# One of four weight sums of a seven-product pair moved from VectorE to an accumulating transfer, with one raw tile less

## The chip, the cores and the metric

The kernel runs on one core of a Trainium2 chip. The metric is the device time of one execution in microseconds (us). The engines are called by the profile's names: PE is TensorE (PEld its weight loads), DVE is VectorE, ACT is ScalarE, POOL is GpSimd, and SP is the engine that issues most transfers.

## The reference, cut to what matters

One layer of a decoder on 256 tokens of width 2048 in float32. Attention and a state-space branch come first; the change lies in the feed-forward part, whose matrices hold most of the weights:

```python
hf = rms_norm(x, g_ffn_norm[i])                                     # 256 x 2048
x = x + (jax.nn.silu(hf @ w_gate[i]) * (hf @ w_up[i])) @ w_down[i]  # 2048 x 5632, twice, and 5632 x 2048
gate = jax.nn.sigmoid(rms_norm(x, g_ple_norm[i]) @ w_ple_gate[i])   # 2048 x 2048
x = x + gate * (p[i] @ w_ple_proj[i])
```

## The kernel before, in words

**Products.** PE multiplies in a rounded 32-bit format. To keep the accuracy, each weight tile and each activation is split into a rounded part `hi` and the rest `lo`, and each product is made of three matmuls (hi by hi, hi by lo, lo by hi). ACT makes `hi` by a copy, DVE makes `lo` by a subtraction (lines 200 and 201).

**Weights.** The class `Weights` holds one list of tiles ("chunks") of 256 rows by 512 columns, 512 KB each, in the order in which PE needs them. `load_to` issues their loads on SP's queue (line 174), `split_to` makes `hi` and `lo`, and `take` hands a chunk to PE while it splits three chunks ahead and loads as many more as there are raw tiles. A raw tile `w_raw` comes from a ring of five; in the gate and up stage two more, `w_more`, take their turn at chunk numbers that leave 0 or 3 after division by seven, so that seven tiles rotate until block 8. A raw tile comes free when ACT and DVE have read it, and only then can SP issue the next load into it.

**Gate and up stage.** There are 11 blocks of 512 columns. A block goes over eight pairs j = 0 to 7; pair j is a chunk g of `w_gate` and a chunk u of `w_up` with the same rows. Each chunk has two halves of 128 rows: g0, g1, u0, u1. A plain pair takes eight products (24 matmuls). The pairs 2, 3, 5 and 6 (in block 0 only 3, 5, 6) are "mixed": seven products (21 matmuls) give the same result, if four sums of weight halves and some sums of activations are at hand. `mix` makes them on DVE:

- `raws[0]` (tile `w_sum_3477`) gets g0 + u0 and u0 + u1,
- `raws[1]` (`w_sum_3478`) gets (g0 + u0) + u1 and that + g1,
- u1 alone is split into `w_last`, and each of the two sum tiles into `w_mix`, hi by ACT and lo by DVE (lines 219, 220; the sums are line 216).

There are two sets of `w_last` and `w_mix` (`NSET` = 2), but one pair of sum tiles. The down stage does the same in four column blocks with the mixed rows 3, 5, 8, 13, 15, 17, 20; of 57 mixed pairs 43 lie in the gate and up stage and 14 in the down stage.

**Between blocks.** The result of a block lies in four PSUM tiles `acc` and four `pp_p`. `shared` and the lines behind `mixed_block` bring them together in `wsg` and `uc` on DVE and ACT (ten DVE instructions of 512 columns a block), and PE then transposes `wsg` to `pp_g` for the down stage. There are two `wsg` tiles, used in turn. Until DVE has read an `acc` tile, PE can't start the next block's sums in it.

**Order.** Instructions are recorded in program order, and a scheduler places them on the engines' queues; weight work is lifted ahead of other work by a fixed priority. Each engine then works its own queue in order and waits by semaphores. POOL's queue carries few transfers: among them the residual rows `xs`, kept in DRAM as `x_keep` during the stage and fetched back, and the last stage's input `pr32`.

The functions that the change touches:

Of the kernel before, what the change touches and what calls it, by code (L numbers as in the profile page):

```python
# [15 lines left out]
ALU = mybir.AluOpType  # L16
# [126 lines left out]
class Weights:  # L143
# [4 lines left out]
    def __init__(self, tc, pool, sched):  # L148
        self.tc, nc = tc, tc.nc
        self.nc, self.pool, self.sched, self.chunks = nc, pool, sched, []  # L150
        self.raw, self.part, self.n_dma, self.n_split = {}, {}, 0, 0
        self.extra, self.native = {}, set()
        self.mixed, self.kept, self.sums, self.more = set(), {}, deque(), deque()

    def block(self, w, k0, nk, c0, n):
        ids = []
# [9 lines left out]
    def load_to(self, i):  # L166
        while self.n_dma <= min(i, len(self.chunks) - 1):
            w, k, c0, n = self.chunks[self.n_dma]
            if self.more and self.n_dma % 7 in (0, 3) and self.n_dma < self.more_end:
                self.more.rotate(1)  # L170
                t = self.more[0]
            else:
                t = self.pool.tile([128, 2, n], F32, tag="raw", bufs=self.RAW, name="w_raw")
            self.nc.sync.dma_start(
                out=t, in_=w[k * 128:(k + 2) * 128, c0:c0 + n].rearrange("(k p) n -> p k n", p=128)
            )
            self.raw[self.n_dma] = t
            self.n_dma += 1
            for out, in_ in self.extra.pop(self.n_dma, ()):
                self.nc.sync.dma_start(out=out, in_=in_)  # L180

    def split_to(self, i):
        while self.n_split <= min(i, len(self.chunks) - 1):
            self.load_to(self.n_split)
            n = self.chunks[self.n_split][3]
            raw = self.raw.pop(self.n_split)
            if self.n_split in self.mixed:
                self.part[self.n_split] = self.mix(self.kept.pop(self.n_split - 1), raw)
                self.n_split += 1
                continue  # L190
            if self.n_split + 1 in self.mixed:
                self.kept[self.n_split] = raw
            if self.n_split in self.native:
                self.part[self.n_split] = (raw, None, 0.0)
                self.n_split += 1
                continue
            hi = self.pool.tile([128, 2, n], F32R, tag="w_hi", bufs=self.PART, name="w_hi")
            lo = self.pool.tile([128, 2, n], F32R, tag="w_lo", bufs=self.PART, name="w_lo")
            with self.tc.high_priority(W_AHEAD):
                self.nc.scalar.activation(out=hi, in_=raw, func=AF.Copy)  # L200
                self.nc.vector.tensor_tensor(out=lo, in0=raw, in1=hi.bitcast(F32), op=ALU.subtract)  # L201
            s = self.sched
            s.act += 2 * n * 0.83e-3 + 0.19
            s.dve = max(s.dve + 2 * n * 1.05e-3 + 0.06, s.act)
            self.part[self.n_split] = (hi, lo, s.dve)
            self.n_split += 1

    def mix(self, g, u):


        V, A, s = self.nc.vector, self.nc.scalar, self.sched
        last, raws, parts = self.sums[0]
        self.sums.rotate(1)

        def add(o, a, b):
            V.tensor_tensor(out=o, in0=a, in1=b, op=ALU.add)  # L216

        def part(h, l, r):
            A.activation(out=h, in_=r, func=AF.Copy)  # L219
            V.tensor_tensor(out=l, in0=r, in1=h.bitcast(F32), op=ALU.subtract)  # L220

        with self.tc.high_priority(W_AHEAD):
            add(raws[0][:, 0], g[:, 0], u[:, 0])
            add(raws[0][:, 1], u[:, 0], u[:, 1])
            part(last[:, 0], last[:, 1], u[:, 1])
            add(raws[1][:, 0], raws[0][:, 0], u[:, 1])
            add(raws[1][:, 1], raws[1][:, 0], g[:, 1])
            for r, (h, l) in zip(raws, parts):
                part(h, l, r)
        s.act += 5 * 512 * 0.83e-3 + 3 * 0.19  # L230
        s.dve = max(s.dve + 9 * 512 * 1.05e-3 + 0.42, s.act)
        (h0, l0), (h1, l1) = parts
        return ((last[:, 0], last[:, 1]), (h0[:, 0], l0[:, 0]), (h0[:, 1], l0[:, 1]),
                (h1[:, 0], l1[:, 0]), (h1[:, 1], l1[:, 1])), None, s.dve
# [16 lines left out]
def hybrid_layer_kernel(  # L251
# [1140 lines left out]


    lhs_f = tiles4(fh, fl)
    wsg = wait_n(2, [128, 2, 512], "wsg")
    uc = wait_get([128, 2, 512], "uc")
    w_sum = wait_n(2, [128, 2, 512], "w_sum")
    for _ in range(NSET):
        W.sums.append((wait_get([128, 2, 512], "w_last", F32R), w_sum,
                       [wait_n(2, [128, 2, 512], "w_mix", F32R) for _ in range(2)]))  # L1400
    W.more_end = blk["gu"][8][0][1]
    W.more.extend(wait_n(2, [128, 2, 512], "w_more"))
    more = list(W.more)
    gr, gh, gl = [], [], []
    lhs_g = tiles4(gh, gl)
# [1 line left out]
    def gate_task(b):  # L1407
        h = yield from S.get([128, 4, 256], "g")
        gr.append(h)
        f2 = lambda a: a.rearrange("p k n -> p (k n)")  # L1410
        for i0 in range(0, 4, 2):
            pt = yield from pp_get("g")
            for i in range(2):
                for t in range(2):
                    transpose(quarter(pt, 2 * i + t), wsg[b % 2][:, t, (i0 + i) * 128:(i0 + i) * 128 + 128])
            yield None
            act(f2(h[:, i0:i0 + 2]), pt, AF.Copy)
            PP.put(pt)
        sched.flags.add(f"g{b}")
        yield 1  # L1420
# [58 lines left out]
            if n > 2000:  # L1479
                raise RuntimeError("no bank")  # L1480

    def mixed_block(ids, lhs, rows, a, b, need):
        acc = accs2() + accs2()
        pq, left = None, sum(i[2] in W.mixed for i in ids)
        n = left
        for i, (j, cg, cu) in enumerate(ids):
            need(j)
            m = cu in W.mixed
            if m and pq is None:
                pq = [wait_pp("p") for _ in range(4)]  # L1490
# [9 lines left out]
    for b in range(11):  # L1500
        if b == 9:
            S.put(*more)
        if b == 10:
# [18 lines left out]
        if b == 2:  # L1522
            keep = [dram.tile([128, 1024], F32, name="x_keep") for _ in range(4)]
            for i in range(4):
                nc.gpsimd.dma_start(out=keep[i], in_=xs[i // 2][i % 2])
                S.put(xs[i // 2][i % 2])
    S.put(*fh, *fl, *rows.values(), wsg[1])
    for i in range(4):
        xs[i // 2][i % 2] = t = wait_get([128, 1024], "xs")
        nc.gpsimd.dma_start(out=t, in_=keep[i])  # L1530
    rows = {}

    def need_g(j):
        last = D_SPLIT if j < 2 * D_SPLIT else 11
        if n == 1 and j == 2 * D_SPLIT - 3:
            split_g(D_SPLIT + 1)
        split_g(min((j + 1) // 2 + 1, last))

# [13 lines left out]
            S.put(gr[i])  # L1552

    ph, pl = [], []
    ws = wsg[0]
    for n, ids in enumerate(blk["down"]):
        p, h = n % 2, n // 2
        acc = mixed_block(ids, lhs_g, rows, ws, uc, need_g)
        with tc.high_priority(G_AHEAD):
            for t in range(2):  # L1560
                tt(ws[:, t], ws[:, t], acc[2 * t], ALU.add)
            for t in range(2):
                tt(uc[:, t], acc[2 * t + 1], uc[:, t], ALU.subtract)
        for c, o in enumerate((ws, uc)):
            for t in range(2):
                stt(xv(t, 2 * p + c), o[:, t], r_f[:, t:t + 1], xv(t, 2 * p + c))
        if n == 3:
            S.put(*gh[D_SPLIT:], *gl[D_SPLIT:], *(rows[j] for j in D_MIXED if j >= 2 * D_SPLIT), *w_sum)
            for last, _, parts in W.sums:
                S.put(last, *parts[0], *parts[1])  # L1570
        if h:
            for b in (2 * p, 2 * p + 1):
                ph.append(wait_get([128, 4, 256], "ph", F32R))
                pl.append(wait_get([128, 4, 256], "pl", F32R))
                sched.add(norm_task(xv, b, ss_p, ph, pl, G_PLE, "hp"), 0)
        if n == 1:
            S.put(*gh[:D_SPLIT], *gl[:D_SPLIT], *(rows[j] for j in D_MIXED if j < 2 * D_SPLIT))
            pr_ = wait_get([128, 2, 2, 256], "prhl", F32R)
            prh, prl = pr_[:, 0], pr_[:, 1]
            pr32 = wait_get([128, 2, 256], "pr32")  # L1580
            nc.gpsimd.dma_start(out=pr32, in_=pT)
            split(prh, prl, pr32)
            S.put(pr32)
    S.put(ws, uc)


# [106 lines left out]
```

## Time and profile before

| | |
|---|---|
| three runs | 1127.79, 1130.6, 1131.61 us (median 1130.6) |
| profiled execution | 1129.42 us, of which 1127.7 us is the span from the first to the last instruction |
| busy share of the span | PE 98%, DVE 88%, ACT 61%, PEld 81%, POOL 2% |
| transfers | 221.18 MB, mean 196 GB/s |
| granted TensorE clock | mean 0.996 of full speed |

Stages by the trace: projections, attention and state-space part up to about 310 us, gate and up stage from there to about 781 us, down stage to about 1030 us, the last projection to the end. The rows of groups read: line, engine, operation, tiles written and read, shapes, count | busy us, mean ns of one | idle time of the engine just before them and what ended it. In a timeline a row gives its start, how long it took, and in brackets the idle time ahead of it. A row of the chain of waits gives the start, the length and what the time went to.

### The profile page before, as it was taken

How to read it: one execution, taken by the hardware profiler on the slowest of the kernel's cores; microseconds unless marked ns; L12 is line 12 of the kernel's file. 1: busy time of each engine (PE TensorE's matmuls, PEld its weight loads, DVE VectorE, ACT ScalarE, POOL GpSimd, SP SyncE). 2: the span in 40 equal slices, each digit the busy share in tenths (PEclk: the TensorE clock that was granted, in tenths of full speed). 3: DMA queues.
4: the chain of work that ended last, by engine and by line, in shares of the span. 5: the costliest groups of instructions: out<-in, count | busy, mean ns of one | idle time of the engine just before them, and what ended most of it. 6: DMA issues, size and time to landing. Idle time of an engine off the chain costs nothing.

```text
span 1127.7 us, 15773 instructions
## 1 busy us (share of the span) xinstructions
PE 1103.1 (98%) x5767; PEld 911.7 (81%) x5767; DVE 987.9 (88%) x1463; ACT 692.8 (61%) x989; POOL 23.3 (2%) x48
## 2 busy tenths in 40 slices
PE   9999999999999999999999999999999999999998
PEld 6877877889887878888888888888888788888886
DVE  7988998657799999999999999999998998978554
ACT  7863993736675765665666665666646555656443
POOL 1000020000000000000000000000000000000000
PEclk9999999999999999999999999999999999999999
DMA  9996460365676566666666556667656565665662
GB/s 337 243 264 205 118 224 20 100 199 183 210 262 200 180 198 205 190 196 208 192 194 207 177 171 204 204 206 244 232 186 222 172 218 190 197 210 167 207 212 88
DMA packets 113342, 221.18 MB, mean 196 GB/s; under 512 B 8160, under 2 KB 13040, under 8 KB 113264
## 3 DMA queue, kind: packets, MB, share of 16 engines
q1 hardware_dynamic: 109808, 211.23, 59.4%
q0 software_dynamic: 3456, 8.94, 2.5%
q8 instruction: 45, 0.74, 0.3%
q14 instruction: 33, 0.27, 0.1%
HBM read 214.76 MB, written 5.37 MB: 195 GB/s over the span
## 4 chain that ended last, share of the span: by engine, by line
PE 46%; DVE 36%; issue 7%; DMA 7%; ACT 3%; DVEq 0%; POOL 0%; SPq 0%; ACTq 0%; POOLq 0%
PE acc L377 37%; DVE w_lo L201 12%; DVE w_sum L216 8%; PE pp_p L377 4%; DVE w_mix L220 4%; DMA w_raw<-in_w_up_dram 4%; DVE w_last L220 2%; DVE uc L361 2%; DVE wsg L361 2%; DMA e<-in_bE_dram 1%; PE pp_at L377 1%; ACT w_hi L200 1%; PE pp_at L1022 1%; DVE w L769 1%; DMA w_raw<-in_w_down_dram 1%
## 5 line engine op out<-in xcount | busy, mean ns | idle before, releaser
L200 ACT ACTIVATE w_hi<-w_raw 128x1024 fp32r<-128x1024 f32 (+2 forms) x299 | 310.6, 1043 | 216.3 <-PE acc L377 166.9
L201 DVE TENSOR_TENSOR w_lo<-w_raw,w_hi 128x1024 fp32r<-128x1024 f32 (+2 forms) x299 | 356.9, 1200 | 78.7 <-ACT w_hi L200 77.9
L219 ACT ACTIVATE w_mix<-w_sum 128x1024 fp32r<-128x1024 f32 x114 | 120.3, 1058 | 84.6 <-DVE w_sum L216 82.9
L377 PE MATMUL acc<-w_hi,fh 128*128 128x512 f32 x403 | 159.1, 395 | 0.7 <-DVE wsg L361 0.5
L377 PE MATMUL acc<-w_lo,fh 128*128 128x512 f32 x403 | 157.5, 391 | 0.8
L377 PE MATMUL acc<-w_hi,fl 128*128 128x512 f32 x403 | 157.1, 390 | 0.0
L220 DVE TENSOR_TENSOR w_mix<-w_sum,w_mix 128x1024 fp32r<-128x1024 f32 x114 | 138.5, 1216 | 0.1
L377 PE MATMUL pp_p<-w_mix,sum 128*128 128x512 f32 x513 | 126.4, 390 | 1.6 <-DVE fl L369 1.1
L377 PEld LDWEIGHTS pp_p<-w_mix,sum 128*128 128x128 f32 x513 | 96.0, 188 | 22.7 <-issue 2.4
L377 PE MATMUL acc<-w_hi,gh 128*128 128x512 f32 x254 | 99.1, 390 | 1.5 <-DVE uc L361 1.5
L377 PE MATMUL acc<-w_hi,gl 128*128 128x512 f32 x254 | 98.8, 389 | 0.0
L377 PE MATMUL acc<-w_lo,gh 128*128 128x512 f32 x254 | 98.8, 389 | 0.0
L377 PEld LDWEIGHTS acc<-w_hi,fh 128*128 128x128 f32 x403 | 75.7, 188 | 18.2 <-DVE uc L361 2.4
L377 PEld LDWEIGHTS acc<-w_lo,fh 128*128 128x128 f32 x403 | 75.7, 188 | 17.7 <-DVE w_lo L201 2.7
L377 PEld LDWEIGHTS acc<-w_hi,fl 128*128 128x128 f32 x403 | 75.6, 188 | 15.7
L216 DVE TENSOR_TENSOR w_sum<-w_raw 128x512 f32<-128x512 f32 x87 | 57.5, 682 | 13.3 <-DMA w_raw<-in_w_up_dram 5.9
L216 DVE TENSOR_TENSOR w_sum<-w_sum,w_raw 128x512 f32<-128x512 f32 x96 | 65.4, 681 | 0.0
L377 PEld LDWEIGHTS acc<-w_hi,gh 128*128 128x128 f32 x254 | 47.7, 188 | 11.8 <-DVE uc L361 1.9
L377 PEld LDWEIGHTS acc<-w_hi,gl 128*128 128x128 f32 x254 | 47.7, 188 | 9.9
L377 PEld LDWEIGHTS acc<-w_lo,gh 128*128 128x128 f32 x254 | 47.7, 188 | 9.7
L219 ACT ACTIVATE w_last<-w_raw 128x512 fp32r<-128x512 f32 x48 | 30.2, 628 | 32.6 <-DMA w_raw<-in_w_up_dram 16.8
L377 PE MATMUL acc<-w_hi,ph 128*128 128x512 f32 x128 | 49.8, 389 | 0.0
(329 smaller groups left out, 2034.5 us busy)
## 6 DMA issues: line engine op xcount, KB each, us to landing
w_raw<-in_w_down_dram SPq DMA_DIRECT2D x88, 512.0 KB, 4.5
w_raw<-in_w_up_dram SPq DMA_DIRECT2D x71, 512.0 KB, 4.5
w_raw<-in_w_gate_dram SPq DMA_DIRECT2D x70, 512.0 KB, 4.5
w_raw<-in_w_o_dram SPq DMA_DIRECT2D x32, 512.0 KB, 4.0
w_raw<-in_w_ple_gate_dram SPq DMA_DIRECT2D x32, 512.0 KB, 4.5
w_raw<-in_w_in_dram SPq DMA_DIRECT2D x24, 512.0 KB, 7.5
w_more<-in_w_gate_dram SPq DMA_DIRECT2D x18, 512.0 KB, 4.3
w_more<-in_w_up_dram SPq DMA_DIRECT2D x17, 512.0 KB, 4.8
```

The costliest lines, as they stand in the source:

```text
L200: self.nc.scalar.activation(out=hi, in_=raw, func=AF.Copy)
L201: self.nc.vector.tensor_tensor(out=lo, in0=raw, in1=hi.bitcast(F32), op=ALU.subtract)
L216: V.tensor_tensor(out=o, in0=a, in1=b, op=ALU.add)
L219: A.activation(out=h, in_=r, func=AF.Copy)
L220: V.tensor_tensor(out=l, in0=r, in1=h.bitcast(F32), op=ALU.subtract)
L361: V.tensor_tensor(out=o, in0=a, in1=b, op=op)
L377: T.matmul(out=o, lhsT=a, rhs=b, start=start, stop=stop)
L769: V.tensor_tensor_scan(out=w, data0=dc, data1=w, initial=0.0, op0=ALU.mult, op1=ALU.add)
L1022: T.matmul(out=o, lhsT=a, rhs=b_, start=False, stop=(i == 1), skip_group_check=True)
```

## The change

In short: u0 + u1 is no longer made by DVE. When the raw load of a mixed u chunk is issued, POOL's queue gets two more transfers into the sum tile's second half: a plain one of u1 and then an accumulating one that adds u0. The sum tile that these write into is doubled (one for each set, `w_sum_3476` and `w_sum_3477`; `w_sum_3478` stays single). Its room comes from the raw tiles (one `w_more` instead of two, at each sixth chunk, so six rotate), and a second saved tile, one `wsg` instead of two, makes up the rest. With one `wsg`, `shared` of block b is recorded after the transposes of block b - 1. The fetch of `xs` is made in two steps, and `pr32` is fetched and split two blocks later.

```diff
     def load_to(self, i):
 ...
-            if self.more and self.n_dma % 7 in (0, 3) and self.n_dma < self.more_end:
+            if self.more and self.n_dma % 6 == 0 and self.n_dma < self.more_end:
 ...
             self.raw[self.n_dma] = t
+            if self.n_dma in self.mixed:
+                o, g = self.sums[0][1][0][:, 1], self.nc.gpsimd
+                self.sums.rotate(1)
+                self.ahead[self.n_dma] = self.sums[-1]
+                g.dma_start(out=o, in_=w[(k + 1) * 128:(k + 2) * 128, c0:c0 + n])
+                g.dma_start(out=o, in_=w[k * 128:(k + 1) * 128, c0:c0 + n], accum_op=ALU.add)
 ...
-    def mix(self, g, u):
+    def mix(self, g, u, bufs):
 ...
-        last, raws, parts = self.sums[0]
-        self.sums.rotate(1)
+        last, raws, parts = bufs
 ...
             add(raws[0][:, 0], g[:, 0], u[:, 0])
-            add(raws[0][:, 1], u[:, 0], u[:, 1])
             part(last[:, 0], last[:, 1], u[:, 1])
 ...
-        s.dve = max(s.dve + 9 * 512 * 1.05e-3 + 0.42, s.act)
+        s.dve = max(s.dve + 8 * 512 * 1.05e-3 + 0.36, s.act)
 ...
-    wsg = wait_n(2, [128, 2, 512], "wsg")
+    ws = wait_get([128, 2, 512], "wsg")
-    w_sum = wait_n(2, [128, 2, 512], "w_sum")
-    for _ in range(NSET):
-        W.sums.append((wait_get([128, 2, 512], "w_last", F32R), w_sum,
+    w_sum = wait_n(NSET + 1, [128, 2, 512], "w_sum")
+    for i in range(NSET):
+        W.sums.append((wait_get([128, 2, 512], "w_last", F32R), (w_sum[i], w_sum[NSET]),
 ...
-    W.more.extend(wait_n(2, [128, 2, 512], "w_more"))
+    W.more.extend(wait_n(1, [128, 2, 512], "w_more"))
 ...
     def mixed_block(...):
             if m and left == 0:
+                if flag is not None:
+                    sched.until(flag)
                 shared(pq, a, b)
 ...
-    for i in range(4):
-        xs[i // 2][i % 2] = t = wait_get([128, 1024], "xs")
-        nc.gpsimd.dma_start(out=t, in_=keep[i])
+    def reload(p):
+        for t in range(2):
+            xs[t][p] = o = wait_get([128, 1024], "xs")
+            nc.gpsimd.dma_start(out=o, in_=keep[2 * t + p])
+    reload(0)
 ...
+        if n == 1:
+            reload(1)
         acc = mixed_block(ids, lhs_g, rows, ws, uc, need_g)
```

(The last part moves the lines that fetch and split `pr32` from the end of down block 1 to the end of down block 3.)

How it moves instructions. First DVE's queue where one block ends and the next begins, at the third boundary of the gate and up stage. In the first rows DVE frees the raw tiles of pair 7; `w_sum_3477` of `w_raw_4732,w_raw_4750` is g0 + u0 of pair 2 of the next block, and `w_raw_4750` is its u chunk. A tile of the ring of five comes back at the fifth raw number after it: SP loads `w_raw_4616, 4649, 4686, 4730, 4732, 4750` in this order, so `w_raw_4750` lies where `w_raw_4616` lay. Before:

```order
L201 TENSOR_TENSOR w_lo_4747<-w_raw_4616,w_hi_4746 128x1024
L201 TENSOR_TENSOR w_lo_4759<-w_more_3490,w_hi_4758 128x1024
L220 TENSOR_TENSOR w_mix_3483<-w_sum_3478,w_mix_3482 128x1024
L201 TENSOR_TENSOR w_lo_4785<-w_raw_4649,w_hi_4784 128x1024
L216 TENSOR_TENSOR w_sum_3477<-w_raw_4732,w_raw_4750 128x512
L361 TENSOR_TENSOR uc_3476<-wsg_3475,pp_p_4632 128x512
L216 TENSOR_TENSOR w_sum_3477<-w_raw_4750 128x512
L361 TENSOR_TENSOR wsg_3475<-uc_3476,pp_p_4633 128x512
L220 TENSOR_TENSOR w_last_3484<-w_raw_4750,w_last_3484 128x512
```

Now the same place; `w_raw_4782` is the u chunk of pair 2, and SP's order (`w_raw_4659, 4671, 4707, 4709, 4752, 4770, 4782`) puts it where `w_raw_4671` lay, the u chunk of pair 7:

```order
L207 TENSOR_TENSOR w_lo_4767<-w_raw_4659,w_hi_4766 128x1024
L225 TENSOR_TENSOR w_mix_3483<-w_sum_3478,w_mix_3482 128x1024
L207 TENSOR_TENSOR w_lo_4779<-w_raw_4671,w_hi_4778 128x1024
L207 TENSOR_TENSOR w_lo_4808<-w_raw_4707,w_hi_4807 128x1024
L221 TENSOR_TENSOR w_sum_3477<-w_raw_4770,w_raw_4782 128x512
L365 TENSOR_TENSOR uc_3475<-wsg_3474,pp_p_4653 128x512
L225 TENSOR_TENSOR w_last_3484<-w_raw_4782,w_last_3484 128x512
L365 TENSOR_TENSOR wsg_3474<-uc_3475,pp_p_4654 128x512
```

Between the instruction that frees the place and the first one that needs the new load stood three instructions of 1024 columns; now one stands there. The row `w_sum_3477<-w_raw_4750` (u0 + u1) is gone. The same holds at six boundaries, those ahead of blocks 2 to 7.

POOL's queue in the gate and up stage. Before, nothing stands there between `x_keep` and the fetch of `xs` near the stage's end:

```order
L1525 DMA x_keep_4517<-xs_2019 128x1024
L1525 DMA x_keep_4518<-xs_2020 128x1024
L1525 DMA x_keep_4519<-xs_2021 128x1024
L1530 DMA xs_7184<-x_keep_4516 128x1024
L1530 DMA xs_7186<-x_keep_4517 128x1024
L1530 DMA xs_7188<-x_keep_4518 128x1024
L1530 DMA xs_7190<-x_keep_4519 128x1024
```

Now two transfers for each mixed pair; in brackets what each waits for (DMASW: the landing of a POOL transfer; DVE, Activation: an instruction there):

```order
L1530 DMA x_keep_4538<-xs_2021 128x1024 [waits DMASW5_49,DVE_49]
L182 DMA w_sum_3476<-in_w_up_dram 128x512 [waits DMASW0_49,DVE_49]
L183 DMA w_sum_3476<-in_w_up_dram 128x512 [waits DMASW6_49,DMASW5_49]
L182 DMA w_sum_3477<-in_w_up_dram 128x512 [waits DVE_49,Activation_49]
L183 DMA w_sum_3477<-in_w_up_dram 128x512 [waits DMASW7_49]
L182 DMA w_sum_3476<-in_w_up_dram 128x512 [waits DMASW6_49,DMASW1_49,DVE_49]
L183 DMA w_sum_3476<-in_w_up_dram 128x512 [waits DMASW2_49,DMASW1_49]
```

The first of two waits until DVE has split the sum tile for the mixed pair before the last one; the second waits for the first one's landing, and whatever follows on POOL waits behind it.

DVE's queue from the split that frees `w_sum_3476` (pair 3 of a block, first row) towards its next split (pair 6). The next two rows behind these are the split of `w_sum_3478` and then `w_mix_3481<-w_sum_3476,w_mix_3480`, which reads the sum that the two transfers made meanwhile:

```order
L225 TENSOR_TENSOR w_mix_3481<-w_sum_3476,w_mix_3480 128x1024
L207 TENSOR_TENSOR w_lo_4656<-w_raw_4551,w_hi_4655 128x1024
L225 TENSOR_TENSOR w_mix_3483<-w_sum_3478,w_mix_3482 128x1024
L207 TENSOR_TENSOR w_lo_4668<-w_raw_4576,w_hi_4667 128x1024
L221 TENSOR_TENSOR w_sum_3477<-w_raw_4603,w_raw_4605 128x512
L225 TENSOR_TENSOR w_last_3484<-w_raw_4605,w_last_3484 128x512
L221 TENSOR_TENSOR w_sum_3478<-w_sum_3477,w_raw_4605 128x512
L225 TENSOR_TENSOR w_mix_3486<-w_sum_3477,w_mix_3485 128x1024
L207 TENSOR_TENSOR w_lo_4695<-w_raw_4603,w_hi_4694 128x1024
L221 TENSOR_TENSOR w_sum_3478<-w_sum_3478,w_raw_4603 128x512
L221 TENSOR_TENSOR w_sum_3476<-w_more_3489,w_raw_4635 128x512
L225 TENSOR_TENSOR w_last_3479<-w_raw_4635,w_last_3479 128x512
```

So between the freeing split and the next one lie six instructions of 1024 columns and six of 512.

More of the change, by code (lines that the diff above doesn't have):

```diff
@@ L152, in __init__ @@
         self.extra, self.native = {}, set()
-        self.mixed, self.kept, self.sums, self.more = set(), {}, deque(), deque()
+        self.mixed, self.kept, self.sums, self.more, self.ahead = set(), {}, deque(), deque(), {}
     def block(self, w, k0, nk, c0, n):
@@ L187, in split_to @@
             if self.n_split in self.mixed:
-                self.part[self.n_split] = self.mix(self.kept.pop(self.n_split - 1), raw)
+                self.part[self.n_split] = self.mix(self.kept.pop(self.n_split - 1), raw, self.ahead.pop(self.n_split))
                 self.n_split += 1
@@ L1414, in gate_task @@
                 for t in range(2):
-                    transpose(quarter(pt, 2 * i + t), wsg[b % 2][:, t, (i0 + i) * 128:(i0 + i) * 128 + 128])
+                    transpose(quarter(pt, 2 * i + t), ws[:, t, (i0 + i) * 128:(i0 + i) * 128 + 128])
             yield None
@@ L1480, in wait_pp, with mixed_block @@
                 raise RuntimeError("no bank")
-    def mixed_block(ids, lhs, rows, a, b, need):
+    def mixed_block(ids, lhs, rows, a, b, need, flag=None):
         acc = accs2() + accs2()
@@ L1508, in hybrid_layer_kernel @@
             S.put(gr[0])
-        ws = wsg[b % 2]
-        acc = mixed_block(blk["gu"][b], lhs_f, rows, ws, uc, need_f)
+        acc = mixed_block(blk["gu"][b], lhs_f, rows, ws, uc, need_f, f"g{b - 1}" if b else None)
         if b == 0:
@@ L1526, in hybrid_layer_kernel @@
                 S.put(xs[i // 2][i % 2])
-    S.put(*fh, *fl, *rows.values(), wsg[1])
-    for i in range(4):
-        xs[i // 2][i % 2] = t = wait_get([128, 1024], "xs")
-        nc.gpsimd.dma_start(out=t, in_=keep[i])
+    S.put(*fh, *fl, *rows.values())
+    def reload(p):
[3 more added lines that the diff above has]
+    reload(0)
     rows = {}
@@ L1535, in need_g @@
         if n == 1 and j == 2 * D_SPLIT - 3:
+            S.put(gh[0], gl[0])
             split_g(D_SPLIT + 1)
@@ L1554, in hybrid_layer_kernel @@
     ph, pl = [], []
-    ws = wsg[0]
     for n, ids in enumerate(blk["down"]):
         p, h = n % 2, n // 2
+        if n == 1:
+            reload(1)
         acc = mixed_block(ids, lhs_g, rows, ws, uc, need_g)
@@ L1570, in hybrid_layer_kernel @@
                 S.put(last, *parts[0], *parts[1])
+            pr_ = wait_get([128, 2, 2, 256], "prhl", F32R)
+            prh, prl = pr_[:, 0], pr_[:, 1]
+            pr32 = wait_get([128, 2, 256], "pr32")
+            nc.gpsimd.dma_start(out=pr32, in_=pT)
+            split(prh, prl, pr32)
+            S.put(pr32)
         if h:
@@ L1576, in hybrid_layer_kernel @@
         if n == 1:
[L1577 to L1583, printed above, removed]
+            S.put(*gh[1:D_SPLIT], *gl[1:D_SPLIT], *(rows[j] for j in D_MIXED if j < 2 * D_SPLIT))
     S.put(ws, uc)
```

## The prediction, made before the run

> **What bounds the kernel now.** The profile's page comes first: the busy shares, and the shares of the chain that ended last.
>
> ```profile
> PE 1103.1 (98%) x5767; PEld 911.7 (81%) x5767; DVE 987.9 (88%) x1463; ACT 692.8 (61%) x989; POOL 23.3 (2%) x48
> PE 46%; DVE 36%; issue 7%; DMA 7%; ACT 3%; DVEq 0%; POOL 0%; SPq 0%; ACTq 0%; POOLq 0%
> ```
>
> PE is busy nearly always, yet less than half of the chain lies on it: DVE holds a third. Two engines run neck and neck, so the average settles nothing, and I go stage by stage, with the view by windows (length, then PE, PEld, DVE, ACT and POOL busy, granted clock, DMA share, GB/s).
>
> ```profile
> 500.00:550.00 50.00, 49.87 (x223) 40.60 (x222) 48.41 (x59) 31.64 (x36) 0.00 (x0) 1.00 0.64 195
> 800.00:850.00 50.00, 50.00 (x222) 41.44 (x221) 46.98 (x59) 27.03 (x31) 0.00 (x0) 1.00 0.61 200
> ```
>
> In the gate and up stage DVE is at 97%, in the down stage at 94%; the clock is full. How much faster could PE go if DVE never kept it waiting? Two chain rows give PE's prices.
>
> ```profile
> 790.00 1.05 PE pp_g L404 x8
> ...
> 818.95 11.56 PE acc L377 x51
> ```
>
> A matmul takes 11.56 / 51 = 0.2267 us. A block has four plain pairs and four mixed ones, 4 x 24 + 4 x 21 = 180 matmuls: 40.8 us, and with eight transposes (1.05) 41.85. The block's actual period is in the chain, where each block boundary shows one load of 512 KB:
>
> ```profile
> 437.61 5.30 DMA w_raw<-in_w_up_dram
> ...
> 480.40 4.99 DMA w_raw<-in_w_up_dram
> ...
> 522.89 5.03 DMA w_raw<-in_w_up_dram
> ...
> 565.41 4.82 DMA w_more<-in_w_up_dram
> ...
> 607.72 5.06 DMA w_raw<-in_w_up_dram
> ```
>
> The boundaries lie 42.79, 42.49, 42.52 and 42.31 us apart. So PE's floor is only 0.5 to 0.9 us a block away. What holds the block at 42.5 is seen in DVE's timeline at the boundary of 480 us:
>
> ```profile
> 479.16 1.22 DVE L201 TENSOR_TENSOR w_lo<-w_raw,w_hi 128x1024 fp32r<-128x1024 f32 x1
> 480.29 1.22 DVE L201 TENSOR_TENSOR w_lo<-w_more,w_hi 128x1024 fp32r<-128x1024 f32 x1
> 481.43 1.22 DVE L220 TENSOR_TENSOR w_mix<-w_sum,w_mix 128x1024 fp32r<-128x1024 f32 x1
> 483.28 1.23 DVE L201 TENSOR_TENSOR w_lo<-w_raw,w_hi 128x1024 fp32r<-128x1024 f32 x1 [0.64 <-ACT w_hi L200]
> 485.42 0.69 DVE L216 TENSOR_TENSOR w_sum<-w_raw 128x512 f32<-128x512 f32 x1 [0.91 <-DMA w_raw<-in_w_up_dram]
> 486.03 0.68 DVE L361 TENSOR_TENSOR uc<-wsg,pp_p 128x512 f32<-128x512 f32 x1
> 486.63 0.68 DVE L216 TENSOR_TENSOR w_sum<-w_raw 128x512 f32<-128x512 f32 x1
> ```
>
> Successive starts give DVE's price: 1.14 us for 1024 columns (480.29 to 481.43), 0.60 for 512 (485.42 to 486.03). The first row frees a raw tile at 480.38; the load into it begins at 480.40 and lands at 485.39; at 485.42 the first sum of pair 2 starts, having waited 0.91. This is a loop: DVE frees, SP loads, DVE waits. Behind that sum in DVE's order stand the evacuations (`uc`, `wsg`) for which PE's next sums wait. SP does not hold back on its own, it waits for freed tiles all the time (us, times, longest):
>
> ```profile
> SPq L174 <- DVE w_lo L201: 550.7, 237, 27.6
> SPq L174 <- DVE w_sum L216: 238.0, 93, 7.2
> ```
>
> **The loop, before and after.** By the code a block gives DVE 20 instructions of 1024 columns (twelve `w_lo`, eight `w_mix`) and 30 of 512 (16 sums, four `w_last`, ten of the evacuation): 20 x 1.14 + 30 x 0.60 = 40.8 us. Three instructions of 1024 columns (3.42) run beside the boundary's load, the rest stands in line with it: 40.8 - 3.42 + 5.03 = 42.41, against 42.49 measured. This closes, so I use it.
>
> After: four sums fewer, 4 x 0.60 = 2.40 off DVE, 38.4 left. But with six raw tiles in place of seven only one instruction stands between the freeing split and the sum that needs the load, so the cover falls from 3.42 to 1.14, by 2.28. The loop becomes 38.4 - 1.14 + L = 37.26 + L, L being the new load's time. Even at L = 5.03 that is 42.29: the 2.40 spared is eaten by the 2.28 of lost cover. That is -0.12 at each of six boundaries (ahead of blocks 2 to 7), -0.7 us. From here everything hangs on L.
>
> **L.** Now POOL's transfers run beside it: pair 3's first one starts when DVE has split the sum tile of pair 6, a row or two ahead of the boundary, so two transfers of 256 KB are under way while this load is. Nothing in the trace shows an accumulating transfer. The nearest rows, chain and POOL timeline:
>
> ```profile
> 696.35 4.51 DMA w_raw<-in_w_up_dram
> ...
> 738.75 4.53 DMA w_raw<-in_w_up_dram
> ...
> 851.95 6.38 DMA w_raw<-in_w_down_dram
> ```
> ```profile
> 851.91 0.54 POOL L1581 DMA_DIRECT2D pr<-in_pT_dram  x1 [63.80 <-PE acc L377]
> ```
>
> At 851.9 a 256 KB transfer of POOL starts with a load of SP, and the load takes 6.38; 696 and 738, with five tiles in the ring, show 4.51 and 4.53. The table of transfers (KB each, median us to landing) and the window in which the DMA engines are fullest give the upper end:
>
> ```profile
> w_raw<-in_w_up_dram SPq DMA_DIRECT2D x71, 512.0 KB, 4.5
> w_raw<-in_w_in_dram SPq DMA_DIRECT2D x24, 512.0 KB, 7.5
> xs<-x_keep POOLq DMA_DIRECT2D x4, 512.0 KB, 4.7
> ...
> pr<-in_pT_dram POOLq DMA_DIRECT2D x1, 256.0 KB, 5.8
> rope<-in_pos_dram POOLq DMA_DIRECT2D x1, 1.0 KB, 3.2
> ```
> ```profile
> 0.00:50.00 50.00, 47.15 (x232) 37.10 (x233) 41.97 (x110) 39.07 (x76) 5.78 (x13) 1.00 0.91 293
> ```
>
> So L lies between 4.5 and 7.5. I take 6.38, the one row with just this neighbour: +1.35 a boundary, six times, +8.1 us. Ends: 6 x (4.5 - 5.03) = -3.2, and 6 x 2.47 = +14.8; below the loop lies PE's floor, which limits the gain to 6 x 0.64 = 3.8.
>
> **Blocks 0, 1, 8 to 10 and the down stage.** There the ring is as before and DVE only gains. What it can give back is what PE waits for DVE (whole run, then 845 to 900 us):
>
> ```profile
> PEld acc L377 <- DVE w_lo L201: 8.7, 12, 1.7
> PEld pp_g L404 <- DVE wsg L361: 4.5, 12, 0.5
> ```
> ```profile
> PEld acc L377 <- DVE uc L361: 1.9, 1, 1.9
> ```
>
> The larger part of the 8.7 lies ahead of 310 us, outside the change. Bounds 0 and -3; I take -1.5, most of the one stall of 1.9.
>
> **POOL's chain.** The second transfer waits for the first one's landing, so one pair takes two in a row. From the split that frees the tile (pair 3) to the split that reads the sum (pair 6) DVE has six instructions of 1024 and six of 512: 6 x 1.14 + 6 x 0.60 = 10.4. ACT first makes `w_mix` of the sum:
>
> ```profile
> L219 ACT ACTIVATE w_mix<-w_sum 128x1024 fp32r<-128x1024 f32 x114 | 120.3, 1058 | 84.6 <-DVE w_sum L216 82.9
> ```
>
> That takes 1.06, so 9.4 us remain for the two. By rows: two like the 1 KB one make 6.4 (3.0 spare), two like `xs` 9.4 (just in time), two like `pr`, the only one of this size, 11.6 (2.2 late). `pr` landed beside a load, as these will now and then; `xs` is twice as large and yet faster. I take the middle, 9.4: 0 us. If it comes late, DVE's `w_mix` waits, and behind it on DVE stand the splits that free raw tiles, so SP's loads are late next.
>
> The Trainium skill, in "DMA: Bandwidth & Descriptors", section "Anatomy of one DMA — SWDGE (gpsimd) path", gives about 2.0 us plus bytes over 436e3 per us, by which a 256 KB transfer takes 2.6 and the pair 5.2 (an estimate from that page), and the chain would never be late; the rows above, 4.7 and 5.8, disagree. Against the change speaks another page, "SBUF — State Buffer", its box on the "DVE blocks DMA" trap: POOL's descriptors are starved while DVE holds the port they share, in its faster modes; whether DVE's sums here do so no row of this case shows, and if they did the chain would be the late one.
>
> **At nothing.** `wsg` single: `shared` of block b comes with its last mixed pair, pair 6, and the transposes of block b - 1 that read the old contents are done by pair 1, five pairs earlier, over 20 us; without that cover PE would wait at `pp_g`, as now by at most 0.5. The two `xs` fetches that stand on POOL ahead of block 10's last sums wait for PE's pair 1; those sums are read from pair 5 on, some 13 us later, and the fetch takes 4.7. `pr32` now waits for PE's pair 13 in the last down block, and its split stands on DVE ahead of a `w_mix` of row 17: between them lie pairs 14 to 16 with 24 + 21 + 24 matmuls, 15.6 us, of which DVE's lead of three chunks takes some 8, and `pr` landed in 5.8; 2 us to spare, and without them PE would wait once for what is missing. The added bytes, 57 x 512 KB = 29.9 MB, move at a DMA share of 0.64. SP's issues keep their number and order.
>
> **Sum** against the profiled execution, 1129.42 us (span 1127.7 and 1.7 around it; 1.2 below the median of 1130.6): 1129.42 - 0.7 + 8.1 - 1.5 + 0 = 1135.3 us.
>
> **Rivals.** 0.3%, about what can be told from no change here, is 3.4 us: below 1127.2 is faster, above 1134.0 slower.
>
> 1. Faster: POOL's transfers don't lengthen the load. For it speaks that the DMA share is only 0.64. At L = 4.5 the loop is 41.76, so PE's floor of 41.85 holds: 6 x (41.85 - 42.49) - 1.5 = -5.3, about 1124. It decides if L stays under 5.0, where the six loops and the 1.5 together reach 1127.2. For it too: one tile less is one load less under way at a time. Against it: the 6.38, and the 4.8 to 5.3 that the boundaries show already with no company. Chance 0.20.
> 2. No change: L between 5.0 and 6.2, spared and lost cover cancel, 1127 to 1134. Chance 0.30.
> 3. Chain late: two transfers like `pr`, 2.2 us at pair 6 of some nine blocks, +20 us, about 1155. It decides from 9.4 us for the two. For it: an accumulating transfer must also read what it adds to, and DVE at 97% has no room for a wait. Against it: four `xs` at 4.7 in mid-run; also the loop of the boundary absorbs part of a late split. Chance 0.20.
> 4. The forecast, L of 6.2 to 7.5 at the boundaries: chance 0.30, 1134 to 1143.
>
> **Range.** From 1125 (most of case 1) to 1152 (the milder part of case 3). Faster 0.20, same 0.30, slower 0.50 (cases 3 and 4).
>
> **What the profile after would show.** DVE's busy time falls by 57 x 0.68 = 39 us, to about 949, from the rows
>
> ```profile
> L216 DVE TENSOR_TENSOR w_sum<-w_raw 128x512 f32<-128x512 f32 x87 | 57.5, 682 | 13.3 <-DMA w_raw<-in_w_up_dram 5.9
> ```
>
> whose count falls by 57. POOL's queue grows from
>
> ```profile
> q0 software_dynamic: 3456, 8.94, 2.5%
> ```
>
> by 29.9 to 38.8 MB. At six boundaries DVE waits L - 1.14, about 5 us instead of 0.9, for the raw tile, and blocks 2 to 7 are 43.6 us apart. If those waits are there but the boundaries stand 42 us apart, L or the loop is wrong; if ACT's `w_mix` waits for a transfer into `w_sum`, case 3 holds; if neither shows and the time still moves, the part that I costed at nothing is at fault.

## The result, and the profile after

| | before | changed |
|---|---|---|
| median of runs | 1130.65 us (1127.79 to 1131.61) | 1173.7 us (1167.98 to 1178.74) |
| span of the profiled execution | 1127.7 us | 1165.8 us |

The ratio is 1.0385, with a 95% interval of 1.0347 to 1.0422: slower by 43 us, far outside the forecast's range. The profiled execution is the fastest of the changed kernel's four (1167.98 us), so the traces below show 38 of the 43 us. The page of the changed kernel, its busy shares, its chain and POOL's queue:

```profile
PE 1113.4 (96%) x5767; PEld 914.9 (78%) x5767; DVE 959.0 (82%) x1406; ACT 687.5 (59%) x989; POOL 104.6 (9%) x162
...
q0 software_dynamic: 16224, 38.83, 14.1%
...
PE 46%; DVE 22%; DMA 15%; issue 11%; ACT 5%; POOL 0%; DVEq 0%; ACTq 0%; SPq 0%; POOLq 0%
```

The change does what it says: DVE has 57 instructions fewer and POOL moves 29.9 MB more. DVE's share of the chain fell from 36% to 22%, and the transfers' share rose from 7% to 15%. Where the 38.1 us between the two spans lie is shown by windows cut at the first evacuation row (`uc<-wsg,pp_p`) of a block: nine blocks (1 to 9), then block 10 with the down stage, then the rest. Before:

```profile
357.20:738.80 381.60, 379.68 (x1690) 309.35 (x1689) 369.87 (x460) 237.88 (x272) 0.00 (x0) 1.00 0.63 194
738.80:1016.40 277.60, 275.34 (x1227) 227.24 (x1226) 255.49 (x323) 165.45 (x192) 2.67 (x5) 1.00 0.63 207
```

The changed kernel, the same work:

```profile
358.60:773.60 415.00, 389.92 (x1695) 315.37 (x1695) 351.15 (x415) 234.82 (x272) 50.41 (x71) 0.98 0.75 225
773.60:1054.60 281.00, 276.54 (x1226) 226.39 (x1225) 246.38 (x306) 163.26 (x192) 26.40 (x38) 1.00 0.75 235
```

The nine blocks take 33.4 us more, block 10 and the down stage 3.4, what lies ahead 1.4, the end nothing. What DVE waits for in the nine blocks (us, times, longest), before:

```profile
DVE w_sum L216 <- DMA w_raw<-in_w_up_dram: 6.7, 7, 1.5
DVE w_lo L201 <- ACT w_hi L200: 3.7, 7, 0.9
DVE w_sum L216 <- DMA w_more<-in_w_up_dram: 1.3, 2, 0.7
```

and after:

```profile
DVE w_sum L221 <- DMA w_raw<-in_w_up_dram: 33.2, 9, 5.9
DVE w_mix L225 <- ACT w_mix L224: 18.6, 10, 2.7
DVE w_lo L207 <- ACT w_hi L206: 9.9, 9, 3.4
```

By these rows DVE waits 61.7 us in place of 11.7, and it is busy 18.7 us less (369.87 to 351.15): +31.3 of the 33.4. Two waits carry most of it: the boundary's load, and the split of a sum (`w_mix`), which waited for nothing before. One turn of the loop in the chain:

```profile
446.60 7.07 DMA w_raw<-in_w_up_dram
...
475.31 5.01 issue
480.33 0.01 POOLq L182
480.34 6.12 DMA w_sum<-in_w_up_dram
...
494.74 6.67 DMA w_raw<-in_w_up_dram
...
528.61 5.51 DMA w_sum<-in_w_up_dram
...
542.40 6.19 DMA w_raw<-in_w_up_dram
```

and in the timelines of DVE, POOL and ACT (cut to the rows named below):

```profile
445.35 1.22 DVE L207 TENSOR_TENSOR w_lo<-w_raw,w_hi 128x1024 fp32r<-128x1024 f32 x1
447.36 1.23 DVE L207 TENSOR_TENSOR w_lo<-w_more,w_hi 128x1024 fp32r<-128x1024 f32 x1 [0.80 <-ACT w_hi L206]
453.69 0.69 DVE L221 TENSOR_TENSOR w_sum<-w_raw 128x512 f32<-128x512 f32 x1 [5.10 <-DMA w_raw<-in_w_up_dram]
...
473.24 1.22 DVE L225 TENSOR_TENSOR w_mix<-w_sum,w_mix 128x1024 fp32r<-128x1024 f32 x1
...
487.66 1.23 DVE L225 TENSOR_TENSOR w_mix<-w_sum,w_mix 128x1024 fp32r<-128x1024 f32 x1 [2.70 <-ACT w_mix L224]
```
```profile
474.75 0.56 POOL L182 DMA_DIRECT2D w_sum<-in_w_up_dram  x1 [2.38 <-DVE w_mix L225]
480.34 0.86 POOL L183 DMA_DIRECT2D w_sum<-in_w_up_dram  x1 [5.03 <-DMA w_sum<-in_w_up_dram]
```
```profile
486.56 1.06 ACT L224 ACTIVATE w_mix<-w_sum 128x1024 fp32r<-128x1024 f32 x1 [2.86 <-DMA w_sum<-in_w_up_dram]
```

At 446.60 SP's load starts into the tile that DVE just freed; only one instruction stands beside it, and DVE waits 5.10 us. At 474.46 the split of pair 3 frees the sum tile; POOL sends the first transfer at 474.75, it lands at 480.05; the second goes off at 480.34 and lands 6.12 later, at 486.46. ACT, and behind it DVE, waited for that: 2.70 us at pair 6. By the prediction's loop a block is then 37.26 + 7.07 + 2.70 = 47.0 us; the two loads are 48.1 us apart (446.60 to 494.74), the rest being DVE's small waits for ACT (0.80 us at 447.36, 0.27 at 464.93). The sign that the prediction gave for its third rival, ACT's `w_mix` waiting for a transfer into `w_sum`, is there.

### The profile page after: what moved, and what is told of

It is laid out like the page before. It is cut to its first block, busy times and chain, and to the rows that moved or that the text cites. A ratio compares the mean times of both kernels' runs of the same rounds, so it can differ in the third digit from the quotient of the medians.

```text
span 1165.8 us, 15987 instructions
## 1 busy us (share of the span) xinstructions
PE 1113.4 (96%) x5767; PEld 914.9 (78%) x5767; DVE 959.0 (82%) x1406; ACT 687.5 (59%) x989; POOL 104.6 (9%) x162
## 4 chain that ended last, share of the span: by engine, by line
PE 46%; DVE 22%; DMA 15%; issue 11%; ACT 5%; POOL 0%; DVEq 0%; ACTq 0%; SPq 0%; POOLq 0%
PE acc L381 37%; DMA w_raw<-in_w_up_dram 6%; DVE w_lo L207 6%; DMA w_sum<-in_w_up_dram 5%; DVE w_sum L221 4%; PE pp_p L381 4%; DVE w_mix L225 3%; DVE uc L365 2%; DMA w_raw<-in_w_down_dram 2%; ACT w_hi L206 2%; DVE wsg L365 1%; DMA e<-in_bE_dram 1%; ACT w_mix L224 1%; DMA w_raw<-in_w_in_dram 1%; DVE w_last L225 1%
## 5 line engine op out<-in xcount | busy, mean ns | idle before, releaser
L207 DVE TENSOR_TENSOR w_lo<-w_raw,w_hi 128x1024 fp32r<-128x1024 f32 (+2 forms) x305 | 365.5, 1205 | 85.6 <-ACT w_hi L206 84.4
L206 ACT ACTIVATE w_hi<-w_raw 128x1024 fp32r<-128x1024 f32 (+2 forms) x305 | 315.7, 1042 | 201.6 <-PE acc L381 153.6
L381 PE MATMUL acc<-w_hi,fh 128*128 128x512 f32 x403 | 162.3, 403 | 22.3 <-DVE wsg L365 14.5
L381 PE MATMUL acc<-w_lo,fh 128*128 128x512 f32 x403 | 161.1, 400 | 1.7 <-DVE w_lo L207 1.7
L381 PE MATMUL acc<-w_hi,fl 128*128 128x512 f32 x403 | 160.5, 398 | 0.0
L224 ACT ACTIVATE w_last<-w_raw 128x512 fp32r<-128x512 f32 x57 | 35.9, 630 | 82.9 <-DMA w_raw<-in_w_up_dram 59.6
L221 DVE TENSOR_TENSOR w_sum<-w_sum,w_raw 128x512 f32<-128x512 f32 x105 | 72.2, 688 | 0.0
L221 DVE TENSOR_TENSOR w_sum<-w_raw 128x512 f32<-128x512 f32 x48 | 33.2, 691 | 46.5 <-DMA w_raw<-in_w_up_dram 32.7
L183 POOL DMA_DIRECT2D w_sum<-in_w_up_dram x43 | 37.2, 865 | 208.8 <-DMA w_sum<-in_w_up_dram 193.4
```

Source lines behind the costliest of these rows:

```text
L183: g.dma_start(out=o, in_=w[k * 128:(k + 1) * 128, c0:c0 + n], accum_op=ALU.add)
L381: T.matmul(out=o, lhsT=a, rhs=b, start=start, stop=stop)
```

## The experiments

Each stretch below is 440 to 610 us, in the middle of the blocks with the loop; a row's first count (x) is the PE records in it, so more means faster. Before and changed:

```profile
440.00:610.00 170.00, 169.45 (x754) 137.73 (x754) 163.74 (x200) 105.12 (x121) 0.00 (x0) 1.00 0.64 198
```
```profile
440.00:610.00 170.00, 154.57 (x662) 124.66 (x661) 137.82 (x164) 91.62 (x108) 18.66 (x27) 0.96 0.71 214
```

**One raw tile less, nothing else** (in the kernel before):

```diff
-            if self.more and self.n_dma % 7 in (0, 3) and self.n_dma < self.more_end:
+            if self.more and self.n_dma % 6 == 0 and self.n_dma < self.more_end:
...
-    W.more.extend(wait_n(2, [128, 2, 512], "w_more"))
+    W.more.extend(wait_n(1, [128, 2, 512], "w_more"))
```

> The kernel before with one raw tile less (six in turn), DVE still making u0 + u1, no new transfer. Theory of the prediction (ring): six tiles leave less of DVE's work beside the boundary's load, the loop grows by up to 2.28 us at six boundaries, so up to 1144 us. Rival (order): what stands beside the load is set by DVE's queue, and in this kernel's queue eight instructions, 5.28 us, stand between the split that frees the tile and the sum that needs the load, more than a load of 5.0 us takes; then no boundary waits and the time is 1126 to 1132 us.

Measured 1128.13 us, ratio 0.9993 (0.998 to 1.0007). The stretch and DVE's only wait in it:

```profile
440.00:610.00 170.00, 169.46 (x763) 140.02 (x762) 166.43 (x202) 105.08 (x122) 0.00 (x0) 1.00 0.65 203
```
```profile
DVE w_lo L201 <- ACT w_hi L200: 2.6, 4, 0.9
```

DVE waits for no load at all, with a tile less. Seven instructions stand beside the boundary's load at 482 us (the expectation counted eight), 2 x 1.14 + 5 x 0.60 = 5.28 us. So the cover that the prediction saw shrink (3.42 to 1.14) didn't shrink for want of a tile alone: it goes with the order of DVE's queue, which is another one in the changed kernel. Which part of the change turned the order, no run separates.

**The raw tile given back, the transfers kept** (the two lines above the other way round, in the changed kernel):

> The changed kernel with the raw tile given back (seven in turn). Ring: the boundary wait of 5 us falls by 2.3 at six boundaries, so about 1160 us. Order: its DVE queue still has one instruction (1.14 us) beside the boundary's load, so that wait stays at 5 us and the time at 1170 to 1176 us.

Measured 1145.29 us, ratio 1.0133 (1.0104 to 1.0162): neither theory. DVE's waits in the stretch:

```profile
DVE w_sum L221 <- DMA w_raw<-in_w_up_dram: 10.0, 3, 4.7
DVE w_lo L207 <- ACT w_hi L206: 4.1, 6, 0.9
DVE w_sum L221 <- DMA w_more<-in_w_up_dram: 3.8, 2, 3.6
```

The boundary's wait is still there, 2.5 to 4.7 us each, but no split waits for a sum. The order of DVE's queue accounts for it: counted in this stretch at 1.14 and 0.60 us an instruction, the shortest stretch between the split that frees a sum tile and the next split of that tile is 13.9 us of work, against 10.4 in the changed kernel, and two transfers of 11.7 and ACT's 1.06 fit into the one and not the other. By this count the tile helps by the order that comes with it; that this is all it does is not shown (see the run with three sum tiles and seven raw tiles).

**One transfer or none.** Three kernels, from the changed one: the plain transfer alone, the accumulating one alone, neither. They leave out u0, u1 or both from the sum; in the last two its half is zeroed once.

```diff
-                g.dma_start(out=o, in_=w[(k + 1) * 128:(k + 2) * 128, c0:c0 + n])
-                g.dma_start(out=o, in_=w[k * 128:(k + 1) * 128, c0:c0 + n], accum_op=ALU.add)
```

> The changed kernel with the plain transfer alone (the accumulating one left out, so u0 isn't added). Chain theory: one transfer of 5.5 us fits into the 9.4 us there are, DVE's wait of 2.6 us a block at the split of the sum goes, and with half the traffic the boundary's load falls from 6.7 to some 5.8 us: 1140 to 1150 us. Rival (traffic is all): only the load's time matters, the split's wait was spent beside the boundary's wait, and it stays near 1160 us.

> The changed kernel with the accumulating transfer alone (the plain one left out, the sum's second half set to zero once, so u0 is added to what stands there). Chain theory: one transfer of 5.8 us has 9.4 us; nothing is late, as with the plain one alone (1128.4): 1127 to 1133 us. Theory of the accumulation: most of the loss comes with it even alone, over 1145 us.

> The changed kernel with neither transfer (the sum tile's second half is set to zero once, u0 + u1 left out). What is left of the change is the order, six raw tiles, one wsg and four DVE sums less a block. By the loop of the prediction, 37.26 + 5.03 = 42.29 us a block: 1126 to 1130 us, so that all of the loss comes with the transfers. Rival: the order or the single wsg cost something by themselves, over 1135 us.

| kernel | us | ratio to before (95%) |
|---|---|---|
| neither | 1125.5 | 0.9962 (0.9942 to 0.9981) |
| plain alone | 1128.4 | 0.9988 (0.9972 to 1.0003) |
| accumulating alone | 1135.7 | 1.0054 (1.0034 to 1.0074) |
| both (the change) | 1173.7 | 1.0385 (1.0347 to 1.0422) |

The stretch with neither and DVE's two longest waits in it, then the stretch with the plain one and with the accumulating one, each with its POOL queue and its landing time:

```profile
440.00:610.00 170.00, 169.83 (x762) 139.95 (x761) 155.87 (x185) 104.25 (x121) 0.00 (x0) 1.00 0.66 203
...
DVE w_lo L205 <- ACT w_hi L204: 10.5, 4, 2.6
DVE w_sum L219 <- DMA w_raw<-in_w_up_dram: 1.0, 2, 0.6
```
```profile
440.00:610.00 170.00, 170.00 (x767) 141.10 (x766) 156.07 (x185) 106.07 (x123) 8.61 (x16) 1.00 0.71 228
...
q0 software_dynamic: 8016, 23.88, 6.9%
...
w_sum<-in_w_up_dram POOLq DMA_DIRECT2D x43, 256.0 KB, 4.2
```
```profile
440.00:610.00 170.00, 169.30 (x755) 138.35 (x754) 155.38 (x185) 103.83 (x121) 14.00 (x16) 1.00 0.75 224
...
q0 software_dynamic: 11664, 23.88, 10.6%
...
w_sum<-in_w_up_dram POOLq DMA_DIRECT2D x43, 256.0 KB, 5.7
```

All that the change does besides the transfers (six raw tiles, one `wsg`, `xs` in two steps, `pr32` later, four DVE sums less), taken together, costs nothing and gains 0.4%: PE stands at its floor. The plain transfer adds 0.26% to that (the intervals overlap), the accumulating one 0.92%. Together that would be 1.2% above 0.9962; the change is 4.2% above it. About three quarters of the loss arise only where both are there, in this kernel one behind the other.

Both expectations for the plain transfer alone were too high, and the accumulating one alone came out between its two. What stands at the boundary goes with that. DVE's order is that of the changed kernel, with one instruction beside the load; but DVE also waits 2.6 us for ACT's `w_hi` there, while the load runs, and the load is short. It takes 4.1 us in the mean of the six boundaries with neither transfer, 3.9 with the plain one, 4.5 with the accumulating one, and 6.3 with both. The lost cover costs something only once the load is long.

**Two in a row, both plain** (`accum_op` left out, so u0 replaces u1):

> The changed kernel with the second transfer plain too: u0 overwrites u1 in the sum tile instead of being added. It still waits for the first one's landing. Chain theory: what costs is that two transfers stand in a row; two plain ones take some 5 + 5 us instead of 11.7, DVE's wait at the sum's split is still there but smaller, 1140 to 1165 us. Theory of the accumulation: what costs is the DMA engines' time of the accumulating bytes (by queue shares 5.8 us of all 16 engines per MB against 3.3 for plain POOL bytes), which makes SP's loads late; without it 1128 to 1135 us.

Measured 1151.35 us, ratio 1.0192 (1.0156 to 1.0227). DVE's waits in the stretch:

```profile
DVE w_sum L221 <- DMA w_raw<-in_w_up_dram: 12.1, 4, 3.6
DVE w_mix L225 <- ACT w_mix L224: 5.9, 4, 2.4
```

Two transfers cost half of the loss without any accumulation; that the second one accumulates makes it twice as bad. Both theories hold in part. Whether the row or the doubled bytes cost that half, this run doesn't separate.

**A third tile for the transferred sum**, so that a pair's transfers may start one mixed pair earlier; the bytes are the same:

```diff
+                (last, both, parts), first = self.sums[0], self.firsts[0]
+                o, g = first[:, 1], self.nc.gpsimd
...
+                self.firsts.rotate(1)
+                self.ahead[self.n_dma] = (last, (first, both), parts)
...
+    w_sum = wait_n(NSET + 2, [128, 2, 512], "w_sum")
+    W.firsts.extend(w_sum[1:])
```

> The changed kernel with three tiles in turn for the transferred sum in place of two (until block 9), so that a pair's transfers may start one mixed pair earlier, some 8 us more for them; the bytes are the same. Chain theory: DVE's wait of 2.6 us a block at the sum's split goes, and with the transfers away from the boundary's load that falls to 5 or 6 us: 1130 to 1148 us. Theory of the accumulation (engine time, whenever it is spent): the loads stay at 5.7 us in the middle and the boundary wait at 5 us: 1155 us or more.

Measured 1150.01 us, ratio 1.0194 (1.0166 to 1.0221). In the changed kernel the stretch has

```profile
DVE w_sum L221 <- DMA w_raw<-in_w_up_dram: 20.7, 4, 5.9
DVE w_mix L225 <- ACT w_mix L224: 10.3, 5, 2.7
```

and with the third tile

```profile
DVE w_lo L212 <- ACT w_hi L211: 10.5, 4, 2.6
DVE w_sum L226 <- DMA w_raw<-in_w_up_dram: 8.7, 4, 2.6
```

The time lies between the ranges of the two theories. The wait at the sum's split is gone. The boundary's wait fell from some 5.2 to 2.2 us, but most of that has only moved: 2.6 us of it stand a row earlier, in `w_lo`'s wait for ACT, beside the same load, which takes 6.0 us in the mean of these four boundaries in place of 6.7. POOL's transfers run beside it here too. So a sum in time takes away half of the loss, 1.9 of 3.85%. The other half goes with the added transfers and not with a late sum. The spans of this kernel and of the one with neither transfer differ by 22.6 us: 12.3 of them lie in the six blocks with the loop, where the boundary's load takes 5.8 us in the mean in place of 4.1, and 7.2 in block 10.

**Third sum tile and seven raw tiles:**

> Three sum tiles in turn and seven raw tiles. Chain theory: better than either alone (1145.3 with seven raw tiles), no wait at the sum's split and more loads ahead: 1127 to 1138 us. Theory of the accumulation: with seven raw tiles DVE's waits at the sum's split were gone already in the gate and up stage, so a third sum tile gains nothing more: 1142 to 1148 us.

Measured 1142.16 us, ratio 1.0124 (1.0094 to 1.0154), against 1.0133 with seven raw tiles alone. As the second theory had it, nothing is left for the third tile to gain; 1.2% stays with the transfers. Read the other way, from 1.0194 to 1.0124, the seventh raw tile takes 0.7% off although no sum was late without it: it does more than give the sum its time. What, no run shows.

**The sum on POOL, no transfer** (in `mix` of the changed kernel):

```diff
+            self.nc.gpsimd.tensor_tensor(out=raws[0][:, 1], in0=u[:, 0], in1=u[:, 1], op=ALU.add)
```

> The changed kernel with no transfer at all; u0 + u1 is made by an addition on POOL, 57 times 128x512. If POOL does this in one to two us beside DVE without slowing it, nothing waits for it (the sum's split comes some 10 us of DVE's work later) and the time is that of the kernel with neither transfer: 1124 to 1128 us, 0.2 to 0.5% below the kernel before. Rival: POOL's additions slow DVE's own (its 128x512 sums take 0.68 us now) or hold the raw tiles longer, and it ends at 1130 us or more.

Measured 1186.58 us, ratio 1.0503 (1.0473 to 1.0532), slower than the change. POOL's group, two moments of its timeline,

```profile
L226 POOL TENSOR_TENSOR w_sum<-w_raw 128x512 f32<-128x512 f32 x57 | 159.8, 2812 | 543.5 <-DMA w_raw<-in_w_up_dram 292.4 <-DMA w_raw<-in_w_down_dram 190.3 <-ACT w_hi L203 16.9
```
```profile
464.51 1.28 POOL L226 TENSOR_TENSOR w_sum<-w_raw 128x512 f32<-128x512 f32 x1 [5.70 <-DMA w_raw<-in_w_up_dram]
477.59 8.46 POOL L226 TENSOR_TENSOR w_sum<-w_raw 128x512 f32<-128x512 f32 x2 [11.80 <-DMA w_raw<-in_w_up_dram]
```

and DVE's timeline at the first of them, then the last row of DVE before it rests in the second, and the next one:

```profile
464.09 0.67 DVE L363 TENSOR_TENSOR uc<-acc,uc 128x512 f32<-128x512 f32 x1
464.69 2.25 DVE L363 TENSOR_TENSOR wsg<-wsg,uc 128x512 f32<-128x512 f32 x2
...
482.97 0.68 DVE L218 TENSOR_TENSOR w_sum<-w_sum,w_raw 128x512 f32<-128x512 f32 x1
485.93 1.23 DVE L222 TENSOR_TENSOR w_mix<-w_sum,w_mix 128x1024 fp32r<-128x1024 f32 x1 [2.28 <-ACT w_mix L221]
```

The two engines hold each other up. At 464.5 POOL's addition takes 1.28 us, and two instructions of DVE at the same time 2.25 in place of some 1.3. The row at 477.6 holds two additions, 7.20 and 1.30 us long: DVE goes on without a gap at its usual 0.68 and 1.21 until its queue comes to rest at 483.65, and the first addition ends 1.15 us behind that. So it is throughout: 43 of the 57 additions take 1.3 to 2.7 us, and each of the other 14, which take 4.8 to 9.2, ends 1.15 us after DVE's last instruction, with DVE at rest. DVE is busy 982.9 us over the whole run, 957.7 in the kernel with neither transfer. So the rival holds (DVE loses 25 us), and what neither theory had comes on top: the long additions. DVE's split at pair 6 waits for them as it did for the transfers.

**One raw tile more in the kernel before** (`% 8 in (0, 3, 6)`, three `w_more`):

> The kernel before with one raw tile more (eight in turn until block 8). Loop theory: in its DVE queue at least 3.4 to 4.6 us stand beside the boundary's load of 5 us, so the boundary wait of 0.9 us shrinks by half or goes, and blocks come down from 42.5 towards PE's floor of 41.85: 1126 to 1129 us. Rival: as with six tiles (0.9993 of before), the number of raw tiles is worth nothing either way: 1128 to 1131 us.

Measured 1127.07 us, ratio 0.9975 (0.9959 to 0.9991): inside the loop theory's range, and 0.25% below the kernel before. That the boundary's wait is the reason isn't shown, since six raw tiles had taken that wait away too (0.9993). Its stretch:

```profile
440.00:610.00 170.00, 169.81 (x762) 139.58 (x761) 167.18 (x206) 105.55 (x123) 0.00 (x0) 1.00 0.67 204
```

## Why the prediction was wrong

The step that failed is POOL's chain, put at 0 us: the two transfers take 11.7 us where 9.4 were free, and DVE's split of the sum waits 18.6 us for them in the nine blocks. A run in which no sum is late is without half of the loss. The other half goes with the added traffic, of which the prediction had only the boundary's load (8.1 us) and put the rest at nothing.

- **The loop of frees, load and wait** was right in form: 37.26 + L, with L = 7.07 and the late sum, gives 47.0 of the changed kernel's measured 48.1. Without transfers the blocks came to 41.7 to 42.0 in the stretch, PE's floor.
- **L** was right: 6.38 was taken, 5.0 to 7.1 measured at the six boundaries, 6.3 in the mean. Part of that is luck: it rested on one row, and the base was off. With neither transfer the load takes 4.1 us, not 5.03, so the transfers lengthen it by 2.2 and not by 1.35. The boundary wait was forecast at about 5 us and is 4.6 to 5.9 in five of the six.
- **The reason for the lost cover** was wrong: six raw tiles leave 5.28 us beside the load when DVE makes the sum. The cover had been read from the queue correctly and put down to a part of the change that doesn't bring it alone.
- **POOL's chain is the term that was mis-sized.** Between 6.4, 9.4 and 11.6 the middle was taken, "just in time". Measured at the place shown: 5.3 and 6.1, with the gap 11.7 us. DVE's splits waited 2.1 to 2.7 us for it in each of blocks 1 to 7 (in blocks 5 and 6 two splits together) and 1.0 in block 8. The one row of the same size (`pr`, 5.8 us) was the right one; preferring a transfer of twice the size because it was faster was the mistake. In the kernel before, the four transfers of `xs` took 3.8 us with no load of SP beside it and 4.4 to 6.3 with one to three; `pr` had three. The rival that named this mechanism priced it at 20 us; DVE's wait at that split is 18.6.
- **Even that rival**, at 1155, fell 13 us short of the profiled execution. Some 8 of them lie in the six blocks of the loop: they grew by 3.5 to 5.5 us, 4.7 in the mean, not by 1.2 + 2.2 = 3.4. The sum is a little later, and DVE's waits for ACT's `w_hi` (3.7 to 9.9 us over the nine blocks), for which the loop has no term, grew too. Most of the rest is block 10 with the down stage, where the forecast had a gain of 1.5 us and 3.4 were lost; block 10 alone grew by 3.9.
- **DVE's relief** was overrated in busy time (39 us forecast, 28.9 measured: 987.9 to 959.0; the forecast took 0.68 us a row, but rows overlap, and by the 0.60 from start to start it is 34), and almost nothing of it could be had anyway beyond PE's floor: with neither transfer the gain is 0.4%, 4 us.
- **Costed at nothing** and, taken together, shown to be so where no transfer stands beside them, in the kernel with neither: one `wsg`, the two-step `xs`, `pr32`. In the changed kernel the first fetch of `xs`, in block 10, takes 7.2 us (4.7 was taken), the sum's plain transfer beside it 7.4, and the chain runs through that transfer. The added bytes, costed at nothing too, were not: with three sum tiles, when no sum is late, 1.9% of loss are left.
- **The Trainium skill's figure** ("DMA: Bandwidth & Descriptors", section "Anatomy of one DMA — SWDGE (gpsimd) path") of 2.6 us for 256 KB (an estimate from that page) fits no transfer of the changed kernel: the shortest plain one took 3.0, the middle one of the plain transfers 5.3. What the Trainium skill's box on descriptors starved by DVE says ("SBUF — State Buffer", section "SBUF: two separate sides") isn't what happened: the plain transfers in the gate and up stage that ran with DVE over 90% busy took 5.0 us in the middle (27 of them), those with DVE 60 to 90% busy 6.1 (11). The Trainium skill, "SBUF — State Buffer", section "Who interferes with whom", says that DVE's two-input `tensor_tensor` has no two-port mode, the kind of mode that the box is about; that agrees.

PE's clock carries little of the loss. It is granted at 0.96 in the stretch of the changed kernel and at 0.99 to 1.00 in the other kernels: behind four of the six boundaries' waits PE runs at half speed for 3.4 us or more (460.1 to 463.5 in the turn shown). But DVE hardly rests then. In that turn it waits for ACT or PE 1.1 us of 48.1, and over the nine blocks 11.3 us in place of 3.7, so by DVE's account at most 7.6 of the 33.4 us can have come that way.

Not settled: how the remaining half, the cost of the added traffic, divides into engine time and mere company. No run has two transfers that don't wait for each other.

## What to carry to other kernels

Work taken off a busy engine is worth only the distance to the next bound, here 0.4%, and must not come back as a wait: before a sum is handed to two dependent transfers, lay their time, taken from transfers of that size in company like theirs, against the work between the instruction that frees the place and the one that reads it. Where a margin lies between the bounds of a price, the late end deserves the larger chance, since DVE, 97% busy here, couldn't make up a wait. After such a change read anew in the queue's order what covers each load; it can move with instructions that have nothing to do with the load.

## What the runs showed of the hardware that was not expected

- An accumulating byte costs the DMA engines nearly twice a plain one. From the queue shares above: plain 6.9% of 1123.5 us less 2.5% of 1127.7 is 49.3 us of all 16 engines for 14.94 MB, 3.3 us a MB; accumulating 10.6% of 1133.1 less the same is 91.9 us, 6.15 us a MB. The packets per transfer rise from 80 to 144.
- A POOL transfer takes the longer, the more loads of SP it meets (in part because a longer one meets more): with the plain one alone, 3.2 us in the middle with no load of SP beside it (9 of them), 4.3 with one (26), 4.9 with two (11); the accumulating one 4.9 with one (16), 5.7 with two (25), 6.4 with four (8).
- An addition of two 128x512 tiles on POOL takes 1.3 to 2.7 us in 43 of 57 cases, and in the other 14 it lasts 4.8 to 9.2 us, until 1.15 us after DVE has come to rest: in those a run of DVE instructions without a gap held it up as a whole. The Trainium skill, "SBUF — State Buffer", section "Who interferes with whom", says that a two-input operation of DVE contends with GpSimd's reads, and the trace agrees: 2.8 us an addition in the mean, and 25 us more on DVE for 57 of them.
